# Scale and shift of the context rows, table powers and hold factors read from PSUM; all squares of x summed by TensorE

## The chip, the cores and the metric

One core of one Trainium2 chip runs the whole program. The metric is device time in microseconds (us). The five engines of a core are TensorE (PE: matmuls, and PEld for its weight loads), VectorE (DVE), ScalarE (ACT), GpSimd (POOL) and SyncE (SP, which here only issues DMAs). Each runs its own instructions in program order; semaphores order them against each other. SBUF is the large working memory. PSUM has 8 banks of 512 fp32 columns on 128 partitions; column c of the buffer `PS` lies in bank c // 512.

## What is computed

One layer of a generator over 1024 latent tokens and 256 context tokens of 1024 channels. Its token mixer is a state-space layer (S5) in both directions: 64 groups of 16 channels, 64 complex states each. The part that matters here:

```
mod = silu_c @ ada_w[i] + ada_b[i]                       # shift, scale, gates (6 x 1024)
xn  = rmsnorm(x, norm1_g)   * (1 + sc1)  + sh1           # latent rows
cn  = rmsnorm(ctx, norm1_g) * (1 + csc1) + csh1          # context rows
lam_bar = exp(lam * dt);  B_bar = (lam_bar - 1) / lam * B    # zero-order hold
h_t = lam_bar * h_{t-1} + B_bar u_t                      # scan; the latent scan starts from the context's end
y   = Re(C h);  out = gelu(y + d_skip * u);  GLU with glu_w;  x += g1 * out
x  += g2 * (relu(h @ w1 + b1)^2 @ w2 + b2)               # h from rmsnorm and the second modulation
```

The MLP is 1024 x 4096 twice, and its products take most of the time after the scan.

## The kernel before

Tokens are taken in chunks of 8, so the scan runs over 128 latent and 32 context chunks, 160 columns in all. Channels lie on partitions in 8 blocks j of 8 groups. x stands as `xu(j)`, 128 x 1280 per block (8 groups of 160 columns), context in the first 16 columns of each half. The first 300 us do the following.

1. **Sums of squares.** `squares(j)` (ScalarE, L148) squares a block into one of four buffers that `sqb` names; `sum_squares(j)` (TensorE, L154) adds it up into `ssq`, in PSUM bank 1, by 8 matmuls, each two rows in the trace. Two pairs of squares are first added by GpSimd (L174), so that six blocks go through TensorE. VectorE makes the token scale `R` of the sums (L314 to L322; `R` is in bank 5), and `scale_x(j)` (L326) applies it.
2. **Hold factors and B_bar.** L199 to L207 make two 128 x 64 factors; `b_bar` (L219 to L226) applies them to B in two pieces of 8 instructions (44 groups, then 20). ScalarE copies powers of lam_bar out (`pt` and `pg`, L193 to L210), and L261 on VectorE waits for the last of these.
3. **Tables.** `e_products(j, half)` (L280 to L284, five 128 x 512 instructions) multiplies powers by B_bar; five of the sixteen halves run on VectorE, the rest on GpSimd. `turn_e` transposes each on TensorE (L294), and ScalarE copies it into the table of block j (L296).
4. **Modulation.** Conditioning products (`cond1`, L301) end in `mb` in bank 7 (L424). VectorE makes the vector `md` (L429, L430), TensorE spreads it over partitions (L433), ScalarE copies it to `mu` (L437). `mod_lat` (ScalarE, L445) and `mod_ctx(j)` (VectorE, L450, two 128 x 256 instructions) apply it.
5. **The loop over j.** `states(j, g)` (TensorE, L488 to L490, one call for each of 8 groups; ScalarE copies out at L491 and L492), then `ups(j)` on VectorE: the upper steps of the scan tree (L466 to L469), with `mod_ctx(j + 2)` at its end. The first piece of `ups(j)` needs groups 0 to 3, the second groups 4 to 7. Between groups stand `turn_e` of later tables, `mod_lat(j + 1)`, and `cond2_next` (L401: four matmuls of the other conditioning columns into bank 7 from 512 KB that ScalarE's queue loads), at the places in `C2AT`: after groups 3 and 7 for j < 3, after 7 for j = 3, after 1, 4 and 6 later. In j = 5 to 7 `k_blocks`, `k_mm` and `k_evac` add other tables, and VectorE's `k_finish` (L578 to L581, three 16 x 128 instructions) closes one; SP then stores it.
6. **The scan** follows at L265, on VectorE, then gates, GLU and MLP on TensorE.

The order of each engine's work is the order of the Python text. Where two engines touch one PSUM bank, the program's semaphores order them. The loop of item 5 reads:

```
    for j in range(8):
        for g in range(8):
            states(j, g)
...
            if (j, g) in C2AT:
                cond2_next()
        mc = mod_ctx(j + 2) if j + 2 < 8 else []
        chained(ups(j), mc)
```

Of the kernel before, what the change touches and what calls it, by code (L numbers as in the profile page):

```python
# [10 lines left out]
OP = mybir.AluOpType  # L11
# [32 lines left out]
DVE_E = ((0, 0), (0, 1), (1, 0), (1, 1), (2, 0))  # L44
# [3 lines left out]
def kernel(ctx, tc, cst, bc, x, xl, ada_w, glu_w, w1, w2, out):  # L48
    nc = tc.nc
    V, S, P, PE, SP = nc.vector, nc.scalar, nc.gpsimd, nc.tensor, nc.sync  # L50
# [6 lines left out]
    UT = sp.tile([128, 2560], F32, name="UT")  # L57
# [3 lines left out]
    E2 = [sp.tile([128, 2048], F32, name=f"E2_{j}", tag=f"r2_{j}") for j in range(8)]  # L61
    PS = pp.tile([128, 4096], F32, name="PS")
# [6 lines left out]
    def vw(ap, *dims):  # L69

        if len(dims) == 1:
            return ap
        names = "abcdef"[:len(dims)]
        return ap.rearrange("p (%s) -> p %s" % (" ".join(names), " ".join(names)),
                            **{names[i]: dims[i] for i in range(len(dims))})

    def size(dims):
        n = 1
        for d in dims:
            n *= d  # L80
        return n

    def at(tile_, off, *dims):
        return vw(tile_[:, off:off + size(dims)], *dims)

    def sb(off, *dims):
        assert R3 + off + size(dims) <= R3 + NR3
        return at(T, R3 + off, *dims)

    def bank(i, n=512, o=0):  # L90
        return PS[:, 512 * i + o:512 * i + o + n]
# [6 lines left out]
    def C(name, *dims):  # L98
        o, k = CO[name]
        return at(T, o, *(dims or (k,)))  # L100
# [14 lines left out]
    ETM = 8192  # L115
# [4 lines left out]
    def xu(j, *dims):  # L120
        return at(X1, XU + 1280 * j, *(dims or (8, 2, 80)))
# [20 lines left out]
    exb = C("ex")[:, None, :].to_broadcast([128, 64, NPOW])  # L142
    ssq = bank(1, 160)
    sqt = [at(E2[5], 0, 1280), at(E2[6], 0, 1280), at(E2[7], 0, 1280), at(X0, 2048, 1280)]
    sqb = (0, 1, 2, 3, 1, 3, 0, 2)

    def squares(j):
        S.activation(sqt[sqb[j]], xu(j, 1280), AF.Square)  # L148

    def sum_squares(j):  # L150

        a = vw(sqt[sqb[j]], 8, 160)
        for g in range(8):
            PE.matmul(ssq, C("sel"), a[:, g], start=(j, g) == (0, 0), stop=(j, g) == (7, 7))  # L154
# [13 lines left out]
    V.scalar_tensor_tensor(kk, ang, -1.0, ang, op0=OP.mult, op1=OP.max)  # L168
    S.activation(tb, ang, AF.Sin)
    S.activation(kk, kk, AF.Sin, scale=-1.0, bias=hpi)  # L170
    for j in (0, 2):
        squares(j)
        squares(j + 1)
        P.tensor_tensor(sqt[sqb[j]], sqt[sqb[j]], sqt[sqb[j + 1]], op=OP.add)  # L174
        sum_squares(j)
    V.tensor_scalar(sc, sc, 1.0, None, op0=OP.add)
    V.reciprocal(sc, sc)
# [2 lines left out]
    q = [at(UT, KT + 192 + 64 * i, 64) for i in range(6)]  # L180
# [8 lines left out]
    pt = [sb(PT + 512 * i, 64, 8) for i in range(3)]  # L189
# [5 lines left out]
    for j in range(4, 8):  # L195
        squares(j)
        sum_squares(j)

    V.tensor_scalar(q[0], pwr[:, :, 1], 1.0, None, op0=OP.subtract)  # L199
    V.tensor_tensor(q[3], pwi[:, :, 1], aim, op=OP.mult)  # L200
    V.tensor_tensor(q[2], q[0], are, op=OP.mult)
    V.tensor_tensor(q[4], pwi[:, :, 1], are, op=OP.mult)
    V.tensor_tensor(q[2], q[2], q[3], op=OP.add)
    V.tensor_tensor(q[3], q[0], aim, op=OP.mult)
    V.tensor_tensor(q[2], q[2], q[1], op=OP.mult)
    V.tensor_tensor(q[4], q[4], q[3], op=OP.subtract)
    V.tensor_tensor(q[3], q[4], q[1], op=OP.mult)  # L207
    for i, pw in ((0, pwr), (1, pwi)):
        S.copy(pg[i][fw], pw[fw, :, 0:8])
        S.copy(pg[i][bw], pw[bw, :, 7::-1])  # L210
    br, bi, bd_, bs = (sb(o, 64, 16) for o in (BR, BI, S1, S2))

    def b_bar(a, b):

        gs = slice(a, b)
        n = b - a
        kre, kim = (q[i][:, gs, None].to_broadcast([128, n, 16]) for i in (2, 3))
        t1, t2 = (at(E2[4], 704 * i, n, 16) for i in range(2))
        V.tensor_tensor(t1, br[:, gs], kre, op=OP.mult)  # L219
        V.tensor_tensor(t2, bi[:, gs], kim, op=OP.mult)  # L220
        V.tensor_tensor(bd_[:, gs], bi[:, gs], kre, op=OP.mult)
        V.tensor_tensor(bi[:, gs], br[:, gs], kim, op=OP.mult)
        V.tensor_tensor(br[:, gs], t1, t2, op=OP.subtract)
        V.tensor_tensor(bi[:, gs], bi[:, gs], bd_[:, gs], op=OP.add)
        V.tensor_tensor(bs[:, gs], br[:, gs], bi[:, gs], op=OP.add)
        V.tensor_tensor(bd_[:, gs], bi[:, gs], br[:, gs], op=OP.subtract)  # L226

    b_bar(20, 64)
    V.tensor_tensor(pt[2], pt[0], pt[1], op=OP.add)
    b_bar(0, 20)  # L230


# [3 lines left out]
    TA, TB = 2432, 2960  # L236
# [34 lines left out]

    def e_products(j, hlf):

        eng, tm = (V, at(UT, 0, 5, 512)) if (j, hlf) in DVE_E else (P, sb(ETM, 5, 512))
        er, ei, t = (vw(tm[:, i], 4, 16, 8) for i in (2 * hlf, 2 * hlf + 1, 4))
        gs = slice(8 * j + 4 * hlf, 8 * j + 4 * hlf + 4)
        sh = [128, 4, 16, 8]
        pr, pi, ps_ = (v[:, gs, None].to_broadcast(sh) for v in pt)
        b, d, s = (v[:, gs, :, None].to_broadcast(sh) for v in (br, bd_, bs))
        eng.tensor_tensor(ei, ps_, b, op=OP.mult)  # L280
        eng.tensor_tensor(t, pi, s, op=OP.mult)
        eng.tensor_tensor(er, ei, t, op=OP.subtract)
        eng.tensor_tensor(t, pr, d, op=OP.mult)
        eng.tensor_tensor(ei, ei, t, op=OP.add)  # L284
        return er, ei

    def e_turn(j, hlf, er, ei):
        for pr_ in range(2):
            b = bank(2 + nev[0] % 2)
            nev[0] += 1  # L290
            for gg in range(2):
                g = 2 * pr_ + gg
                for c, e in ((0, er), (1, ei)):
                    PE.transpose(b[:, 128 * (2 * gg + c):128 * (2 * gg + c) + 128],  # L294
                                 e[:, g].rearrange("p h t -> p (h t)"), ident)
            S.copy(at(E2[j], 256 * (4 * hlf + 2 * pr_), 512), b)  # L296
# [9 lines left out]
    def pool_products(j, hlf):  # L306
        pool_e[j, hlf] = e_products(j, hlf)

    R = bank(5, 160, 256)

    v_, r_, t_ = (at(GX, 160 * i, 160) for i in range(3))

# [4 lines left out]
    def token_scale():  # L317
# [3 lines left out]
        V.tensor_tensor(t_, t_, r_, op=OP.mult)  # L321
        V.scalar_tensor_tensor(R, t_, 1.5, r_, op0=OP.add, op1=OP.mult)  # L322

    def scale_x(j):
        xv = xu(j, 8, 160)
        V.tensor_tensor(xv, xv, R[:, None].to_broadcast([128, 8, 160]), op=OP.mult)  # L326

    tp = {}

    def dve_products(j, hlf):  # L330
        tp[j, hlf] = e_products(j, hlf)

    def turn_e(j, hlf):
        e_turn(j, hlf, *(tp if (j, hlf) in DVE_E else pool_e)[j, hlf])
# [47 lines left out]
    def aw2(n):  # L382
        if n in C2X:
            return at(GX, 0, 1024)
        if n >= C2C and n % 3 == C2C % 3:
            return at(X0, 2048, 1024)
        return sb(AW2[n % 2 if n < C2C else (n - C2C) % 3 - 1], 1024)

    def load_aw2(n, eng=SP):
        if n < 32:  # L390
            part, k = 2 + n // 8, n % 8
            eng.dma_start(out=aw2(n), in_=ada_w[128 * k:128 * k + 128, 1024 * part:1024 * part + 1024])
# [41 lines left out]
    mu = at(T, CO["sel"][0], 8, 2, 8, 2)  # L434
    load_aw2(0)
    load_aw2(1)
    S.copy(mu, vw(bank(6, 256), 8, 2, 8, 2))  # L437
    turn_e(5, 0)
    pool_products(6, 0)
    scale_x(3)  # L440
# [5 lines left out]

    def mod_ctx(j):
        xv = xu(j)[:, :, :, 0:16]
        sc_, sh_ = (mu[:, :, i, j, 1:2][:, :, :, None].to_broadcast([128, 8, 2, 16]) for i in (1, 0))
        return [lambda: V.tensor_tensor(xv, xv, sc_, op=OP.mult), lambda: V.tensor_tensor(xv, xv, sh_, op=OP.add)]  # L450

    def save_u(j):
# [97 lines left out]
    def ksr(j, o, *dims):  # L550
        r = 32 + 64 * (j % 2)
        return sb(KS + o, *dims)[r:r + 16]
# [22 lines left out]
    def k_finish(j, eng=V):  # L575

        k0, kf, dj = ksr(j, 0, 8, 15, 16)[:, :, 7], ksr(j, 1920, 8, 16), ksr(j, 2048, 8, 16)
        eng.tensor_tensor(dj, ident[32:48, None, 32:48].to_broadcast([16, 8, 16]),  # L578
                        C("dg")[32:48, 8 * j:8 * j + 8, None].to_broadcast([16, 8, 16]), op=OP.mult)
        eng.tensor_tensor(kf, kf, dj, op=OP.add)  # L580
        eng.tensor_tensor(k0, k0, kf, op=OP.add)  # L581
        kd = KD[j].rearrange("(h t g c) -> t h g c", h=16, t=8, g=8)
        for t in range(8):
            SP.dma_start(out=kd[t], in_=ksr(j, 0, 8, 240)[:, :, 16 * (7 - t):16 * (7 - t) + 128])  # L584


    for g in range(8):
        mod_lat(0, g)
    woven(mod_ctx(0))
    save_u(0)  # L590
    turn_e(2, 0)
# [81 lines left out]
    for q in range(1, 40):  # L673
        if q - 8 in KSTEP[:-1]:
            k_finish(3 + KSTEP.index(q - 8))
        if q in KSTEP:
            j = 3 + KSTEP.index(q)
# [117 lines left out]
    load_u(0)  # L795
    load_m8(2)
    k_finish(7, P)
    load_u(1)
    load_m8(3)
# [286 lines left out]
    t1, t2, t4 = ([(at(W, o + 1024 * k, 512), at(W, o + 1024 * k + 512, 512)) for k in range(4)] for o in (0, 4096, 8192))  # L1086
# [209 lines left out]
    for u in range(1, 5):  # L1296
        for m in range(21):
            t = 14 * (u - 1)
# [112 lines left out]
    for p in range(7, len(L)):  # L1411
        b, i = L[p]
        t = p - len(L)
# [79 lines left out]
    for d in range(8):  # L1493
        o = acc[:, d, toks[1]]
        S.activation(o, o, AF.Identity, scale=C("fg")[:, d:d + 1])
    rb = norm_rows(r_, 2, toks[1])
    for d in range(8):
        o = acc[:, d, toks[1]]
# [64 lines left out]
```

## Time and profile before

| | us |
|---|---|
| median of 3 runs (1109.08 to 1112.32) | 1109.23 |
| the profiled execution | 1112.36 |
| its span (first to last instruction) | 1110.6 |
| busy: TensorE / VectorE / GpSimd / ScalarE | 953.8 / 917.9 / 607.1 / 552.0 |

Mean granted TensorE clock 0.931 of full speed. Times below are microseconds from the start of the span.

### The profile page before, as it was taken

How to read it: one execution, taken by the hardware profiler on the slowest of the kernel's cores; microseconds unless marked ns; L12 is line 12 of the kernel's file. 1: busy time of each engine (PE TensorE's matmuls, PEld its weight loads, DVE VectorE, ACT ScalarE, POOL GpSimd, SP SyncE). 2: the span in 40 equal slices, each digit the busy share in tenths (PEclk: the TensorE clock that was granted, in tenths of full speed). 3: DMA queues.
4: the chain of work that ended last, by engine and by line, in shares of the span. 5: the costliest groups of instructions: out<-in, count | busy, mean ns of one | idle time of the engine just before them, and what ended most of it. 6: DMA issues, size and time to landing. Idle time of an engine off the chain costs nothing.

```text
span 1110.6 us, 15184 instructions
## 1 busy us (share of the span) xinstructions
PE 953.8 (86%) x5244; PEld 782.1 (70%) x5244; DVE 917.9 (83%) x1393; ACT 552.0 (50%) x1012; POOL 607.1 (55%) x413
## 2 busy tenths in 40 slices
PE   3468676656799989789999999997799999999995
PEld 3337565535688867568888888885578788888885
DVE  8999999999984677789666665656979899999997
ACT  7147475334974456745656454544434243434313
POOL 3787899907373553254423232234858677777803
PEclk9778798776899999899999999998999999999998
DMA  9413354486576601156444535358354363625104
GB/s 383 177 39 129 124 168 132 97 227 190 182 237 208 227 19 47 58 189 199 161 153 139 174 133 180 115 189 283 143 173 140 100 213 87 226 75 174 36 1 152
DMA packets 104637, 168.85 MB, mean 152 GB/s; under 512 B 7664, under 2 KB 61936, under 8 KB 103152
## 3 DMA queue, kind: packets, MB, share of 16 engines
q1 hardware_dynamic: 100128, 153.20, 42.1%
q10 hardware_dynamic: 4432, 14.68, 3.9%
q8 instruction: 41, 0.67, 0.2%
q14 instruction: 36, 0.29, 0.1%
HBM read 120.40 MB, written 47.45 MB: 151 GB/s over the span
## 4 chain that ended last, share of the span: by engine, by line
PE 51%; DVE 28%; ACT 6%; DMA 6%; issue 5%; SPq 1%; POOL 1%; ACTq 0%; DVEq 0%; POOLq 0%
PE PS L773 16%; PE PS L774 16%; PE PS L772 16%; DVE X L469 2%; DMA DY<-X 2%; DVE X L468 2%; DVE z L923 2%; DVE PS L467 1%; DVE PS L466 1%; DVE X L450 1%; SPq L584 1%; DMA T<-DY 1%; DVE PS L699 1%; DVE W L923 1%; ACT T L724 1%
## 5 line engine op out<-in xcount | busy, mean ns | idle before, releaser
L773 PE MATMUL PS<-z,W 128*128 128x512 f32 (+1 forms) x422 | 165.5, 392 | 7.2 <-DVE z L923 7.2
L772 PE MATMUL PS<-z,W 128*128 128x512 f32 (+1 forms) x422 | 165.4, 392 | 0.0
L774 PE MATMUL PS<-z,W 128*128 128x512 f32 (+1 forms) x394 | 153.7, 390 | 0.0
L1343 DVE SCALAR_TENSOR_TENSOR T<-PS,T 128x512 f32<-128x512 f32 x160 | 112.3, 739 | 16.2 <-PE PS L774 13.4
L773 PE MATMUL PS<-W 128*128 128x512 f32 (+1 forms) x254 | 100.0, 394 | 9.8 <-DVE W L923 9.8
L772 PE MATMUL PS<-W 128*128 128x512 f32 (+1 forms) x254 | 99.2, 391 | 2.4 <-ACT W L926 2.4
L773 PEld LDWEIGHTS PS<-z,W 128*128 128x128 f32 x422 | 80.8, 192 | 25.5 <-DVE z L923 9.3
L772 PEld LDWEIGHTS PS<-z,W 128*128 128x128 f32 x422 | 80.7, 191 | 16.3
L774 PE MATMUL PS<-W 128*128 128x512 f32 (+1 forms) x226 | 87.9, 389 | 0.0
L774 PEld LDWEIGHTS PS<-z,W 128*128 128x128 f32 x394 | 75.5, 192 | 15.3 <-DVE W L824 0.2
L923 DVE TENSOR_TENSOR z<-z 128x512 fp32r<-128x512 f32 x57 | 79.2, 1422 | 0.0
L774 PE MATMUL PS<-z,A 128*128 128x512 f32 x198 | 77.0, 389 | 0.0
L923 DVE TENSOR_TENSOR W<-W 128x512 fp32r<-128x512 f32 x52 | 69.8, 1376 | 8.0 <-ACT W L926 8.0
L774 PE MATMUL PS<-W,A 128*128 128x512 f32 x194 | 75.5, 389 | 0.0
L488 PE MATMUL PS<-X,E 128*64 128x160 f32 x256 | 50.8, 341 | 26.6 <-DVE X L450 18.7
L1173 DVE TENSOR_TENSOR T<-T,PS 128x512 f32<-128x512 f32 x64 | 42.9, 685 | 34.7 <-PE PS L774 34.0
L773 PE MATMUL PS<-z,A 128*128 128x512 f32 x170 | 66.2, 390 | 2.1 <-DVE z L923 2.1
L1201 POOL TENSOR_TENSOR T<-T 128x512 f32<-128x512 f32 x25 | 36.1, 1444 | 56.2 <-ACT T L1144 48.1
L772 PE MATMUL PS<-z,A 128*128 128x512 f32 x170 | 66.3, 390 | 0.0
L926 ACT CAST W<-T 128x512 fp32r<-128x512 f32 (+1 forms) x46 | 32.9, 718 | 65.3 <-POOL T L1268 38.9
L773 PEld LDWEIGHTS PS<-W 128*128 128x128 f32 x254 | 48.7, 192 | 23.4 <-DVE W L923 14.1
L923 POOL TENSOR_TENSOR W<-T,W 128x768 fp32r<-128x768 f32 (+1 forms) x24 | 43.6, 1819 | 38.5 <-ACT W L926 38.5
(329 smaller groups left out, 2778.2 us busy)
## 6 DMA issues: line engine op xcount, KB each, us to landing
YD<-T SPq DMA_DIRECT2D x87, 256.0 KB, 2.3
z<-YD SPq DMA_DIRECT2D x57, 256.0 KB, 3.4
W<-YD SPq DMA_DIRECT2D x52, 256.0 KB, 4.8
T<-in_w_dram SPq DMA_DIRECT2D x9, 1024.0 KB, 5.8
T<-in_ada_w_dram ACTq DMA_DIRECT2D x17, 512.0 KB, 4.0
UT<-in_w_dram SPq DMA_DIRECT2D x8, 1024.0 KB, 5.8
T<-in_w_dram SPq DMA_DIRECT2D x20, 384.0 KB, 6.4
UT<-in_w_dram SPq DMA_DIRECT2D x15, 384.0 KB, 4.2
```

The source lines that it names most:

```text
L450: return [lambda: V.tensor_tensor(xv, xv, sc_, op=OP.mult), lambda: V.tensor_tensor(xv, xv, sh_, op=OP.add)]
L468: lambda: eng.tensor_tensor(out_, out_, ta, op=OP.add),
L469: lambda: eng.tensor_tensor(out_, out_, tb_, op=OP.add)]
L488: PE.matmul(b[0:64, c], e[:, g, c, 0:64], uj[:, g], start=True, stop=True)
L772: PE.matmul(o, wt[0], xt[0], start=start, stop=False)
L773: PE.matmul(o, wt[0], xt[1], start=False, stop=False)
L774: PE.matmul(o, wt[1], xt[0], start=False, stop=stop)
L923: eng.tensor_tensor(lo, src, hi.bitcast(F32), op=OP.subtract)
L926: S.copy(vw(to[0][:, 0:size(dims)], *dims) if dims else to[0], src)
L1173: V.tensor_tensor(to, x_, o, op=OP.add)
L1201: P.tensor_tensor(o, x_, z_, op=op)
L1343: V.scalar_tensor_tensor(o, src, g2[:, d:d + 1], o, op0=OP.mult, op1=OP.add)
```

## The change

These values move from SBUF to PSUM: the first two powers tables (`ptv`, two ScalarE copies into bank 1), the products' temporary `t` on VectorE's share, the hold factors (`hold`, bank 7) and two temporaries of `b_bar`, context's scale and shift (`muc`, one more ScalarE copy, bank 7) and `k_finish`'s temporaries (bank 6). `R` moves from bank 5 to bank 7. GpSimd's two adds of squares go; TensorE sums all eight blocks.

```diff
-    sqb = (0, 1, 2, 3, 1, 3, 0, 2)
+    sqb = (0, 1, 2, 3, 0, 1, 2, 3)
...
-    for j in (0, 2):
+    for j in range(4):
         squares(j)
-        squares(j + 1)
-        P.tensor_tensor(sqt[sqb[j]], sqt[sqb[j]], sqt[sqb[j + 1]], op=OP.add)
         sum_squares(j)
...
+    ptv = [vw(bank(1, 160, 160 + 160 * i), 20, 8) for i in range(2)]
+    for i in range(2):
+        S.copy(ptv[i], pt[i][:, 0:20])
+
+    hold = [PS[:, 3616 + 64 * i:3680 + 64 * i] for i in range(2)]
...
-    V.tensor_tensor(q[2], q[2], q[1], op=OP.mult)
+    V.tensor_tensor(hold[0], q[2], q[1], op=OP.mult)
...
-    V.tensor_tensor(q[3], q[4], q[1], op=OP.mult)
+    V.tensor_tensor(hold[1], q[4], q[1], op=OP.mult)
...
-        kre, kim = (q[i][:, gs, None].to_broadcast([128, n, 16]) for i in (2, 3))
-        t1, t2 = (at(E2[4], 704 * i, n, 16) for i in range(2))
+        kre, kim = (h[:, gs, None].to_broadcast([128, n, 16]) for h in hold)
+        t1, t2, t3 = at(E2[4], 0, n, 16), *(vw(PS[:, o:o + 16 * n], n, 16) for o in (1024, 2048))
...
+        t = vw(PS[:, TA:TA + 512] if on_v else tm[:, 4], 4, 16, 8)
...
+        pr, pi, ps_ = (v[:, gs, None].to_broadcast(sh) for v in (*(ptv if on_v else pt[:2]), pt[2]))
...
-    R = bank(5, 160, 256)
+    R = bank(7, 160, 32)
...
+    muc = vw(bank(7, 128, 384), 8, 2, 8)
     S.copy(mu, vw(bank(6, 256), 8, 2, 8, 2))
+    S.copy(muc, vw(bank(6, 256), 8, 2, 8, 2)[:, :, :, :, 1])
...
-        sc_, sh_ = (mu[:, :, i, j, 1:2][:, :, :, None].to_broadcast([128, 8, 2, 16]) for i in (1, 0))
+        sc_, sh_ = (muc[:, :, i, j:j + 1][:, :, :, None].to_broadcast([128, 8, 2, 16]) for i in (1, 0))
...
+        if eng is V:
+            r = 32 + 64 * (j % 2)
+            dj, ks = (vw(PS[r:r + 16, o:o + 128], 8, 16) for o in (3200, 3328))
```

No instruction of the loop changes its place on its engine; what changes there is what it waits for. On TensorE, before, the conditioning matmuls (L401) wait for their load alone, and the first state product of block 3 (its table is `E_3`) is what waits for VectorE, which is to say for `mod_ctx(3)`:

```order
L488 MATMUL PS<-X_69,E_2_72 64x160
L489 MATMUL PS<-X_69,E_2_72 64x2x64
L490 MATMUL PS<-X_69,E_2_72 64x2x16
L401 MATMUL PS<-T 1x256 [waits DMAHW3_49]
L401 MATMUL PS<-T 1x256 x3
L488 MATMUL PS<-X_69,E_3_73 64x160 [waits DVE_49,Activation_49]
```

Now (L401 has become L406, L488 to L490 are L495 to L497) the conditioning matmuls that stand after group 3 of block 2 wait for VectorE as well, and by its count for the second instruction of `mod_ctx(3)`, which reads `muc` in bank 7 and stands at the end of `ups(1)`:

```order
L495 MATMUL PS<-X_69,E_2_72 64x160
L496 MATMUL PS<-X_69,E_2_72 64x2x64
L497 MATMUL PS<-X_69,E_2_72 64x2x16
L406 MATMUL PS<-GX,T 1x256 [waits DMAHW1_49,DVE_49]
L406 MATMUL PS<-GX,T 1x256 x3
L495 MATMUL PS<-X_69,E_2_72 64x160 [waits Activation_49]
```

So the wait for `mod_ctx(3)` has moved forward by half a block: groups 4 to 7 of block 2 now stand behind it. The same holds at six more places, by the semaphore counts: (0, 3) waits for `mod_ctx(1)`, (1, 3) for `mod_ctx(2)`, (3, 7) for `mod_ctx(4)`, (4, 1) for `mod_ctx(5)`, (5, 1) for `mod_ctx(6)` and (6, 1) for `mod_ctx(7)`.

The second place is ScalarE's start, from the second half of the squares (L148) to the copies of powers whose end L261 (now L264) on VectorE waits for. Before:

```order
L148 ACTIVATE E_6_76<-X_69 128x1280 [waits DMAHW6_49,Pool_49]
L148 ACTIVATE X_68<-X_69 128x1280 [waits DMAHW7_49,Pool_49]
L148 ACTIVATE E_5_75<-X_69 128x1280 [waits DMAHW0_49,PE_49]
L148 ACTIVATE E_7_77<-X_69 128x1280 [waits DMAHW1_49,PE_49]
L209 COPY T<-E_2_72 64x512
L210 COPY T<-E_2_72 64x512
L209 COPY T<-UT 64x512
L210 COPY T<-UT 64x512
```

And of the change:

```order
L148 ACTIVATE E_7_77<-X_69 128x1280 [waits DMAHW0_49,PE_49,Activation_49]
L148 ACTIVATE X_68<-X_69 128x1280 [waits DMAHW1_49,PE_49,Activation_49]
L199 COPY PS<-T 128x160 [waits PE_49,Activation_49]
L199 COPY PS<-T 128x160 [waits Activation_49]
L212 COPY T<-E_2_72 64x512
L213 COPY T<-E_2_72 64x512
L212 COPY T<-UT 64x512
L213 COPY T<-UT 64x512
```

The copy to `ptv` (L199), in bank 1 beside `ssq`, waits for TensorE's last sum of squares, and the four copies of powers now stand behind it.

## Rows read from the trace of the kernel before

**Rows 1.** Busy us by stage: PE, PEld, DVE, ACT, POOL; PEclk; DMA share; GB/s.

```profile
85.00:212.00 127.00, 89.31 (x1110) 74.93 (x1112) 117.76 (x192) 74.81 (x250) 112.50 (x96) 0.86 0.43 134
```

**Rows 2.** VectorE's timeline to 64 us: start, duration, line, operation.

```profile
15.07 2.93 DVE L200 TENSOR_TENSOR UT<-UT,T 128x64 f32<-128x64 f32 x1
...
29.85 1.36 DVE L220 TENSOR_TENSOR E<-T,UT 128x320 f32<-128x320 f32 x1
...
41.35 0.71 DVE L261 TENSOR_TENSOR T<-T 128x512 f32<-128x512 f32 x1
...
43.66 1.55 DVE L281 TENSOR_TENSOR UT<-T 128x512 f32<-128x512 f32 x1
```

**Rows 3.** GpSimd's timeline at its first add.

```profile
14.97 2.94 POOL L174 TENSOR_TENSOR E<-E,E 128x1280 f32<-128x1280 f32 x1 [10.40 <-ACT E L148]
```

**Rows 4.** ScalarE's timeline, three places.

```profile
12.48 3.57 ACT L148 ACTIVATE E<-X 128x1280 f32<-128x1280 f32 x3
...
27.37 0.66 ACT L210 COPY T<-UT 64x512 f32<-64x512 f32 x1
...
163.51 0.38 ACT L491 COPY X<-PS 128x264 f32<-128x264 f32 x1
```

**Rows 5.** TensorE's timeline, the last sums of squares.

```profile
28.38 4.51 PE L154 MATMUL PS<-E,T 128*128 128x160 f32 x32
```

**Rows 6.** VectorE's timeline, 75 to 124 us.

```profile
75.26 1.47 DVE L326 TENSOR_TENSOR X<-X,PS 128x1280 f32<-128x1280 f32 x1
...
96.86 0.71 DVE L466 TENSOR_TENSOR PS<-X,PS 128x528 f32<-128x528 f32 x1 [1.04 <-ACT X L491]
...
108.00 0.70 DVE L466 TENSOR_TENSOR PS<-X,PS 128x528 f32<-128x528 f32 x1
...
123.08 0.70 DVE L466 TENSOR_TENSOR PS<-X,PS 128x528 f32<-128x528 f32 x1
```

**Rows 7.** VectorE's timeline, 150 to 212 us.

```profile
150.31 0.70 DVE L466 TENSOR_TENSOR PS<-X,PS 128x528 f32<-128x528 f32 x1
...
163.63 0.70 DVE L466 TENSOR_TENSOR PS<-X,PS 128x528 f32<-128x528 f32 x1
...
177.19 1.25 DVE L578 TENSOR_TENSOR T<-T 16x128 f32<-16x128 f32 x1
...
211.01 0.28 DVE L265 COPY PS<-PS 128x128 f32<-128x128 f32 x1
```

**Rows 8.** VectorE's groups by line and shape, 80 to 212 us: busy, mean ns, idle before.

```profile
L450 DVE TENSOR_TENSOR X<-X,T 128x256 f32<-128x256 f32 x16 | 18.5, 1157 | 0.1
...
L581 DVE TENSOR_TENSOR T<-T 16x128 f32<-16x128 f32 x3 | 3.6, 1199 | 0.2
...
L466 DVE TENSOR_TENSOR PS<-X,PS 128x224 f32<-128x224 f32 x8 | 3.2, 396 | 1.2 <-DVE X L468 0.5
```

**Rows 9.** Waits over 62 to 213 us: total us, times, longest.

```profile
PE PS L401 <- DVE PS L267: 7.5, 1, 7.5
```

**Rows 10.** TensorE's timeline in the loop.

```profile
100.88 0.61 PE L401 MATMUL PS<-GX,T 128*1 128x256 f32 x8
...
104.42 1.09 PE L294 MATMUL PS<-T 128*128 128x128 f32 x8
...
108.23 0.32 PE L488 MATMUL PS<-X,E 128*64 128x160 f32 x1 [2.18 <-DVE X L450]
...
123.31 0.50 PE L488 MATMUL PS<-X,E 128*64 128x160 f32 x1 [6.98 <-DVE X L450]
...
127.90 1.09 PE L294 MATMUL PS<-T 128*128 128x128 f32 x8
...
139.15 1.03 PE L401 MATMUL PS<-T 128*1 128x256 f32 x8
...
152.84 1.03 PE L401 MATMUL PS<-T 128*1 128x256 f32 x8
```

**Rows 11.** TensorE's granted clock: stretch, busy, PEclk, DMA share, GB/s.

```profile
120.00:122.00 2.00, 0.00 (x0) 0.57 0.00 0
```

More of the change, by code (lines that the diff above doesn't have):

```diff
@@ L216, in b_bar @@
         n = b - a
-        kre, kim = (q[i][:, gs, None].to_broadcast([128, n, 16]) for i in (2, 3))
-        t1, t2 = (at(E2[4], 704 * i, n, 16) for i in range(2))
+        kre, kim = (h[:, gs, None].to_broadcast([128, n, 16]) for h in hold)
+        t1, t2, t3 = at(E2[4], 0, n, 16), *(vw(PS[:, o:o + 16 * n], n, 16) for o in (1024, 2048))
         V.tensor_tensor(t1, br[:, gs], kre, op=OP.mult)
         V.tensor_tensor(t2, bi[:, gs], kim, op=OP.mult)
-        V.tensor_tensor(bd_[:, gs], bi[:, gs], kre, op=OP.mult)
+        V.tensor_tensor(t3, bi[:, gs], kre, op=OP.mult)
         V.tensor_tensor(bi[:, gs], br[:, gs], kim, op=OP.mult)
         V.tensor_tensor(br[:, gs], t1, t2, op=OP.subtract)
-        V.tensor_tensor(bi[:, gs], bi[:, gs], bd_[:, gs], op=OP.add)
+        V.tensor_tensor(bi[:, gs], bi[:, gs], t3, op=OP.add)
         V.tensor_tensor(bs[:, gs], br[:, gs], bi[:, gs], op=OP.add)
@@ L272, in e_products @@
     def e_products(j, hlf):
-        eng, tm = (V, at(UT, 0, 5, 512)) if (j, hlf) in DVE_E else (P, sb(ETM, 5, 512))
-        er, ei, t = (vw(tm[:, i], 4, 16, 8) for i in (2 * hlf, 2 * hlf + 1, 4))
+        on_v = (j, hlf) in DVE_E
+        eng, tm = (V, at(UT, 0, 4, 512)) if on_v else (P, sb(ETM, 5, 512))
+        er, ei = (vw(tm[:, i], 4, 16, 8) for i in (2 * hlf, 2 * hlf + 1))
+        t = vw(PS[:, TA:TA + 512] if on_v else tm[:, 4], 4, 16, 8)
         gs = slice(8 * j + 4 * hlf, 8 * j + 4 * hlf + 4)
         sh = [128, 4, 16, 8]
-        pr, pi, ps_ = (v[:, gs, None].to_broadcast(sh) for v in pt)
+        pr, pi, ps_ = (v[:, gs, None].to_broadcast(sh) for v in (*(ptv if on_v else pt[:2]), pt[2]))
         b, d, s = (v[:, gs, :, None].to_broadcast(sh) for v in (br, bd_, bs))
@@ L577, in k_finish @@
         k0, kf, dj = ksr(j, 0, 8, 15, 16)[:, :, 7], ksr(j, 1920, 8, 16), ksr(j, 2048, 8, 16)
+        ks = kf
+        if eng is V:
+            r = 32 + 64 * (j % 2)
+            dj, ks = (vw(PS[r:r + 16, o:o + 128], 8, 16) for o in (3200, 3328))
         eng.tensor_tensor(dj, ident[32:48, None, 32:48].to_broadcast([16, 8, 16]),
                         C("dg")[32:48, 8 * j:8 * j + 8, None].to_broadcast([16, 8, 16]), op=OP.mult)
-        eng.tensor_tensor(kf, kf, dj, op=OP.add)
-        eng.tensor_tensor(k0, k0, kf, op=OP.add)
+        eng.tensor_tensor(ks, kf, dj, op=OP.add)
+        eng.tensor_tensor(k0, k0, ks, op=OP.add)
         kd = KD[j].rearrange("(h t g c) -> t h g c", h=16, t=8, g=8)
```

## The prediction, made before the change was run

> **What bounds the kernel now.** I read busy time by stage first, then VectorE's timeline up to the scan, then what TensorE waits for in the loop over j. From 85 to 212 us VectorE is busy 117.8 of 127 us, TensorE 89.3, GpSimd 112.5 [rows 1]: VectorE sets the pace up to the scan, and GpSimd works beside it nearly all the time. The scan starts at 211.01 [rows 7]; everything behind it is ordered after it, so I take each us that its start moves as one us of the total. All but a few short instructions of the change lie before that point.
>
> Two kinds of VectorE instruction are slow here. With both operands in SBUF they stretch beside GpSimd: L200, 64 columns, takes 2.93 [rows 2] while GpSimd's add takes 2.94 over the same time [rows 3]; a product of 512 columns takes 1.55, L220 of 320 columns 1.36 [rows 2], and the sixteen instructions of `mod_ctx` (L450, 256 columns) 1.157 in the mean [rows 8]. With one operand in PSUM they do not: L466 takes 0.70 or 0.71 for 528 columns [rows 6] and 0.396 for 224 [rows 8], with GpSimd just as busy. So a contended instruction that gets a PSUM operand falls to about 0.72 (512 columns), 0.5 (320), 0.43 (256), estimates from these two widths.
>
> **The change up to the loop.** GpSimd's adds go, so L200 and its twin fall from 2.93 to under 0.3 (as 128 columns take 0.28 [rows 7]): 5.3 us. Five of the contended instructions of `b_bar`'s second piece fall from about 1.36 to 0.5: 4.3. VectorE would be ready for L261 at 41.35 - 9.6 = 31.8 [rows 2].
>
> It cannot go on then. Three squares take ScalarE 3.57 from 12.48, so the first ends at 13.7 [rows 4], and TensorE need no longer wait for the add, which ends at 17.9 [rows 3]. But it has 128 rows to do in place of 96, and 32 rows take 4.51 [rows 5]. Before, 17.9 to 32.9 were 15.0 for 96 rows; now 19.5, ending at 33.2. The two copies to `ptv` wait for that end, since they write the bank of the sums, and ScalarE's four copies of powers stand behind them (0.66 each, before done at 28.0 [rows 4]). With 0.3 for each `ptv` copy (bounds: nothing, or the 0.66 of the wider copy) they end at 36.6. VectorE, 9.6 us ahead, loses 4.9 of it: 4.8 remain.
>
> Five table halves run on VectorE. Beside GpSimd five instructions of about 1.5 become one of 1.5 and four of 0.73: 3.1 less. That holds for the first, third and fifth; the second and fourth ran while GpSimd was idle and gain nothing, and I count 1 us lost on the fourth. Ahead by 4.8 + 3.1 + 3.1 - 1.0 = 10.0. Now two new waits: `scale_x(2)` writes from `R` in bank 7 and waits for the conditioning products there, about 1.6; `scale_x(3)`, which ran at 75.26 [rows 6] with no wait, waits for the copy to `muc`, which comes after `md`, TensorE's spreading matmuls and two copies: 2.9 (both estimates; bounds 2 and 7 together). Left: 5.5. Fifth half: 8.6. `mod_ctx(0)` saves 2 x 0.73 (1.157 less 0.43): 10.1, of which TensorE's last transposes, which had ended before it, take 0.8. The first states come 9.3 earlier, and with them the second piece of `ups(0)`, at 96.86 before [rows 6]: 87.5. This sum has an uncertainty of about 3 us.
>
> **The loop, where it is given back.** From that second piece to the next block's first is 108.00 - 96.86 = 11.1 [rows 6], with two `mod_ctx` instructions in it; now 9.7, so `ups(1)` starts at 97.2. A block in which VectorE waits for nothing took 163.63 - 150.31 = 13.3 [rows 7]; now 11.9.
>
> But the conditioning matmuls in bank 7 now wait for `mod_ctx(j + 2)` of the block before, which is the last thing that VectorE does ahead of `ups(j)`. Behind them on TensorE, in order, stand the remaining groups of block j, whose copies the second piece of `ups(j)` needs. So in j = 1, 2, 4, 5, 6 TensorE no longer works ahead: VectorE ends block j - 1, then TensorE does the rest of block j's groups, then VectorE goes on. The block takes D(j) + 9.7, where D is the time from the matmuls' start to ScalarE's copy of the last group.
>
> That such a wait goes by bank and not by columns is in the trace of before: the same matmuls once waited 7.5 us for L267 on VectorE [rows 9], which reads other columns of bank 7. The Trainium skill ("PSUM — Partial Sum Buffer", section on bank collisions) states the rule that speaks against this change: PSUM is to be guarded by bank and quadrant, since another address of the same bank still collides. By addresses the loop would lose nothing and the total be about 1080; by banks the sum is what follows.
>
> D from rows. With TensorE fast, conditioning takes 0.54 and four groups 3.0 (100.88 to 104.42), 0.75 a group; after an idle stretch conditioning takes 0.96 (1.03 in its row, less overlap) and four groups 4.6 (123.31 to 127.90), 1.15 a group [rows 10]. The clock behind it: granted 0.57 in the mean over 120 to 122, with TensorE idle [rows 11], that is on its way from 2.4 to 1.2 GHz; it was idle 6.98 ahead of 123.31 [rows 10]. In the change TensorE idles 5 to 10 us ahead of each of the five waits, so I take each D with a slow start and a fast end. ScalarE's copies add 0.7.
> - D(1) = 0.96 + 4.0 + 0.7 = 5.7. D(2) has a transposed table more (1.09 in rows 10): 6.7.
> - D(4) has six groups, two slow, and two more conditioning parts: 0.96 + 2 x 1.15 + 4 x 0.75 + 1.2 + 0.7 = 8.2.
> - D(5) stands in the trace, slow start included: 152.84 [rows 10] to ScalarE's copy at 163.51 + 0.38 [rows 4] is 11.05; with the semaphore 11.3. D(6) has the same work.
>
> Starts of `ups(j)`: j = 2 at 97.2 + 5.7 + 9.7 = 112.6 (before 123.08 [rows 6]); 3 at 129.0; 4, without a stall, at 140.9 (150.31); 5 at 158.8 (163.63); 6 at 158.8 + 11.3 + 9.7 = 179.8, where before VectorE was at 177.19 [rows 7]. From there to the scan: 11.3, in which `k_finish(0)` is hidden, 8.9 (9.7 without `mod_ctx`), a `k_finish` of 0.9 (its instructions took 1.199 beside GpSimd [rows 8], alone 0.3), 11.1 and 0.9 again, 33.1: the scan starts at 212.9 against 211.01.
>
> That is 1.9 us later: 1114.3 for the profiled execution, which took 1112.36 and lies 3.1 above the median; against the median of 1109.23 it is **1111**.
>
> **Rivals.**
> 1. *The waits bind, but TensorE stays fast*, or its idle stretches end sooner. D falls by 1.5, 1.5, 1.2, 0.8 and 0.8: 5.8 us, total 1105. For it: after 2.18 us of idle, at 108.23, a state product took 0.32. Against it: after 6.98 it took 0.50 [rows 10].
> 2. *The change does what it says and the waits cost nothing.* Five blocks at 11.9 from 97.2, then 25: scan at 181.7, total 1080. For it: VectorE is busy nearly throughout, so all that is saved there counts. Against it: the order of TensorE's queue and [rows 9].
> 3. *Slower*: TensorE stays slow through all of D, since it now works in short bursts. Every group at 1.15, every conditioning part at 0.96, the tables in j = 5 and 6 likewise: D grows by 0.6, 1.1, 2.3, 2.6 and 2.6, total 1111 + 9 = 1120. It decides from the point where the clock comes back only after the last group. For it: in the stretch after 123.31 four whole groups take 4.6. Against it: the next rows there, 1.09 for the transposes at 127.90, are as fast as at 104.42 [rows 10].
>
> **How the numbers follow.** A run of this kernel tells about 0.3% (3.3 us) from no change: below 1105.9 is faster, above 1112.6 slower. Forecast 0.42, by itself 1107 to 1115; rival 1 0.22, rival 2 0.08, rival 3 0.28. Faster: rival 2, over half of rival 1 and a tail of the forecast, 0.24. Slower: nearly all of rival 3 and a quarter of the forecast, 0.35. Same: 0.41. The range runs from 1098 (rival 1 with 3 us more saved up to the loop and some of rival 2) to 1120; outside it is most of rival 2 and a tail of rival 3.
>
> **What would show it.** L200 at 0.3 and L450's successor at 0.43 show the contention gone; VectorE idle before L264 until ScalarE's copies, near 36.6, shows the first stall; `ups(1)` starts near 97. In the loop VectorE must idle ahead of the second piece in j = 1, 2, 4, 5, 6 for D less the first piece's 2.3, about 30 us in all, released by ScalarE's L498, and TensorE's conditioning matmuls by L457. If VectorE has no such idle time, or the matmuls wait for loads alone, the forecast is wrong; if the idle time is there and the clock in D is full, rival 1; if it is half throughout, rival 3.

## The result: slower by 0.9%, and the profile after

| | before | after |
|---|---|---|
| median, us | 1109.23 | 1120.94 (1115.91 to 1121.58, 5 runs) |
| ratio to before, 95% interval | | 1.0088 (1.0063 to 1.0114) |
| profiled execution / its span, us | 1112.36 / 1110.6 | 1120.36 / 1118.6 |
| start of the scan in the profile, us | 211.01 | 220.92 |

The forecast was 1111, no change or a little slower, with a range from 1098 to 1120. The change costs 11.7 us by the medians and 9.8 by the ratio (0.0088 of 1110). Lines of the changed kernel stand 3 to 11 higher: L261 is L264, L401 is L406, L450 is L457, L466 is L473, L491 is L498, L566 is L573.

The window that answers to [rows 1] (busy us of PE, PEld, DVE, ACT, POOL, then PEclk, DMA share, GB/s):

```profile
85.00:212.00 127.00, 79.20 (x972) 65.65 (x972) 84.00 (x161) 64.11 (x216) 102.73 (x90) 0.80 0.40 124
```

VectorE was busy 117.8 of these 127 us and is now busy 84.0: what it saved stands there as idle time. Its timeline after, with the idle time before an instruction and who ended it in brackets, answers to [rows 2, 6, 7]:

```profile
15.31 0.21 DVE L204 TENSOR_TENSOR UT<-UT,T 128x64 f32<-128x64 f32 x1
...
36.85 1.24 DVE L264 TENSOR_TENSOR T<-T 128x512 f32<-128x512 f32 x1 [5.28 <-ACT T L213]
...
67.95 1.49 DVE L331 TENSOR_TENSOR X<-X,PS 128x1280 f32<-128x1280 f32 x1 [3.30 <-ACT PS L444]
...
102.02 0.71 DVE L473 TENSOR_TENSOR PS<-X,PS 128x528 f32<-128x528 f32 x1 [3.67 <-ACT X L498]
...
119.41 0.71 DVE L473 TENSOR_TENSOR PS<-X,PS 128x528 f32<-128x528 f32 x1 [5.34 <-ACT X L498]
...
149.94 0.71 DVE L473 TENSOR_TENSOR PS<-X,PS 128x528 f32<-128x528 f32 x1 [2.34 <-ACT X L498]
...
172.63 0.71 DVE L473 TENSOR_TENSOR PS<-X,PS 128x528 f32<-128x528 f32 x1 [4.06 <-ACT X L498]
...
182.60 0.35 DVE L589 TENSOR_TENSOR PS<-T 16x128 f32<-16x128 f32 x1
...
196.99 0.71 DVE L473 TENSOR_TENSOR PS<-X,PS 128x528 f32<-128x528 f32 x1 [5.19 <-ACT X L498]
...
220.92 0.30 DVE L268 COPY PS<-PS 128x128 f32<-128x128 f32 x1
```

Read from the top: L204 was L201 before, the twin of the contended L200, and takes 0.21 in place of 2.93. L264 stands still 5.28 us until ScalarE's copies of powers. `scale_x(3)` waits 3.30 for the copy to `muc`. Then the second piece of `ups(j)` waits in j = 1, 2, 4, 5 and 6 (L473, released by ScalarE's copy of a state group), 2.34 to 5.34 us each; in j = 4, 5, 6 the first piece waits too, 3.89, 6.49 and 5.88. `k_finish(0)` starts at 182.60, the scan at 220.92. The waits summed over 28 to 220 us (total, times, longest):

```profile
PE PS L406 <- DVE X L457: 41.6, 6, 10.0
...
DVE PS L473 <- ACT X L498: 40.1, 10, 6.5
...
DVE T L264 <- ACT T L213: 5.3, 1, 5.3
```

TensorE's conditioning matmuls wait 41.6 us for `mod_ctx`, six times, and VectorE then waits 40.1 us for state groups. Of these, 3.3 us fall in j = 0, where the conditioning matmuls did not have to wait, and 36.9 behind the waits in j = 1, 2, 4, 5 and 6; the sixth wait, 1.66 us after (3, 7), holds VectorE up nowhere. Before, L401 waited for VectorE once, 7.5 us [rows 9], and VectorE waited for ScalarE 1.04 us in `ups(0)` [rows 6] and 1.30 us in `ups(7)`.

### The profile page after: what moved, and what is told of

Same layout as the page of the kernel before. It is cut to its first block, busy times and chain, and to the rows that moved or that the text cites. A ratio compares the mean times of both kernels' runs of the same rounds, so it can differ in the third digit from the quotient of the medians.

```text
span 1118.6 us, 15256 instructions
## 1 busy us (share of the span) xinstructions
PE 962.0 (86%) x5276; PEld 789.3 (71%) x5276; DVE 878.4 (79%) x1393; ACT 553.6 (49%) x1015; POOL 590.3 (53%) x411
## 4 chain that ended last, share of the span: by engine, by line
PE 57%; DVE 22%; ACT 8%; DMA 5%; issue 4%; POOL 3%; SPq 1%; DVEq 0%; POOLq 0%; ACTq 0%
PE PS L784 16%; PE PS L785 16%; PE PS L783 16%; DVE X L476 2%; DMA DY<-X 2%; DVE X L475 2%; PE PS L154 2%; PE PS L573 2%; DVE PS L474 2%; DVE PS L473 2%; DVE z L934 1%; PE PS L495 1%; DMA T<-in_ada_w_dram 1%; ACT T L735 1%; PE PS L406 1%
## 5 line engine op out<-in xcount | busy, mean ns | idle before, releaser
L934 DVE TENSOR_TENSOR z<-z 128x512 fp32r<-128x512 f32 x57 | 75.7, 1361 | 0.0
L785 PE MATMUL PS<-W,A 128*128 128x512 f32 x194 | 75.5, 389 | 0.0
L784 PE MATMUL PS<-W,A 128*128 128x512 f32 x166 | 64.6, 389 | 0.0
L783 PE MATMUL PS<-W,A 128*128 128x512 f32 x166 | 64.6, 389 | 0.0
```

What stands on the lines that cost most here:

```text
L783: PE.matmul(o, wt[0], xt[0], start=start, stop=False)
L784: PE.matmul(o, wt[0], xt[1], start=False, stop=False)
L785: PE.matmul(o, wt[1], xt[0], start=False, stop=stop)
L934: eng.tensor_tensor(lo, src, hi.bitcast(F32), op=OP.subtract)
```

## The experiments

Two theories. Theory A: the loss is the wait of the conditioning matmuls for `mod_ctx`, which exists since `muc` lies in their bank; the rest of the change gains. Theory B: the copy in PSUM gains, and the loss comes from the other parts (longer sums on TensorE, copies in ScalarE's queue, the clock).

**The copy in another bank.** Only 96 columns of bank 6 are free through the loop, so six blocks read it and two read SBUF as before the change.

```diff
-    muc = vw(bank(7, 128, 384), 8, 2, 8)
+    muc = vw(bank(6, 96, 416), 8, 2, 6)
-    S.copy(muc, vw(bank(6, 256), 8, 2, 8, 2)[:, :, :, :, 1])
+    S.copy(muc, vw(bank(6, 256), 8, 2, 8, 2)[:, :, :, 0:6, 1])
-        sc_, sh_ = (muc[:, :, i, j:j + 1][:, :, :, None] ...
+        sc_, sh_ = ((muc[:, :, i, j:j + 1] if j < 6 else mu[:, :, i, j, 1:2])[:, :, :, None] ...
```

> The change with the context's scale and shift in bank 6 in place of bank 7, for six of the eight blocks (96 columns are free there; blocks 6 and 7 read SBUF as before the change). Theory (the wait of the conditioning matmuls for mod_ctx, by bank 7, is what was lost): the five stalls of the loop go, VectorE starts ups(1) near 93, since scale_x(3) no longer waits 3.3 us for the copy either, and the scan near 181; total 1083 us (1076 to 1095). Rival (the loss comes from TensorE's clock and the longer sums of squares, whatever bank is read): 1115 to 1122.

Measured 1087.64 us, ratio 0.9795 (0.9781 to 0.9810). TensorE's groups by line, 80 to 188 us (busy, mean ns, idle before):

```profile
L406 PE MATMUL PS<-T 128*1 128x256 f32 x128 | 10.2, 392 | 1.6 <-DMA T<-in_ada_w_dram 1.6
...
L406 PE MATMUL PS<-GX,T 128*1 128x256 f32 x16 | 1.2, 377 | 0.0
```

None of L406's idle time is put down to VectorE any more; it is 1.6 us, for a load. VectorE's timeline:

```profile
63.82 1.49 DVE L331 TENSOR_TENSOR X<-X,PS 128x1280 f32<-128x1280 f32 x1 [1.25 <-PE PS L429]
...
188.18 0.30 DVE L268 COPY PS<-PS 128x128 f32<-128x128 f32 x1
```

`scale_x(3)`'s wait is gone too; `scale_x(2)`'s (63.82) is left. The scan starts at 188.18, 32.7 us sooner than with the copy in bank 7, although two of the eight blocks read SBUF again. The choice of that bank decides the sign of the whole change. Against the estimate of 181 the scan is 7 us late, and the total is 5 us above the 1083 expected, inside the range. The trace shows where most of the 7 us lie, if the prediction's sizes are taken for this part: the second piece of `ups(7)` waits 2.12 us for ScalarE; `k_finish`, whose first instruction stays slow, takes 1.8, 1.5 and 1.6 us where the prediction had 0.9; and `ups(6)` and `ups(7)`, without that wait, take about 11.8 us each where it had 11.1.

```profile
157.53 1.05 DVE L589 TENSOR_TENSOR PS<-T 16x128 f32<-16x128 f32 x1
...
177.05 0.71 DVE L473 TENSOR_TENSOR PS<-X,PS 128x528 f32<-128x528 f32 x1 [2.12 <-ACT X L498]
```

**No copy.** `mod_ctx` reads SBUF as before, the rest of the change stays.

```diff
-    muc = vw(bank(7, 128, 384), 8, 2, 8)
-    S.copy(muc, vw(bank(6, 256), 8, 2, 8, 2)[:, :, :, :, 1])
...
-        sc_, sh_ = (muc[:, :, i, j:j + 1][:, :, :, None] ...
+        sc_, sh_ = (mu[:, :, i, j, 1:2][:, :, :, None] ...
```

> The change without the PSUM copy of the context's scale and shift: mod_ctx reads SBUF as before, all other parts stay. Theory: no stalls in the loop, but mod_ctx takes about 1.16 us an instruction again beside GpSimd; ups(1) near 96, scan near 189, total 1089 us (1083 to 1097). Rival (the other parts lose by themselves): above 1109.

Measured 1095.04 us, ratio 0.9867 (0.9852 to 0.9881): the other parts gain, and theory B's second half falls. The total is 6 us above the one expected, inside its range. `mod_ctx` in that run (its line is L455 there):

```profile
L455 DVE TENSOR_TENSOR X<-X,T 128x256 f32<-128x256 f32 x15 | 17.3, 1154 | 0.1
```

At 1.154 us an instruction it is as slow as before the change [rows 8]; that costs 8 us against the copy in bank 6 (0.9867 - 0.9795 of 1110).

**The copy alone, in bank 7, on the kernel before.**

```diff
+    muc = vw(bank(7, 128, 384), 8, 2, 8)
     S.copy(mu, vw(bank(6, 256), 8, 2, 8, 2))
+    S.copy(muc, vw(bank(6, 256), 8, 2, 8, 2)[:, :, :, :, 1])
-        sc_, sh_ = (mu[:, :, i, j, 1:2][:, :, :, None] ...
+        sc_, sh_ = (muc[:, :, i, j:j + 1][:, :, :, None] ...
```

> The kernel before with that copy in bank 7 alone. Theory: mod_ctx falls to 0.41 us an instruction, the conditioning matmuls wait for it, and without the gains of the other parts the loop's loss stands alone: scan near 232, total 1128 us (1122 to 1134). Rival (the copy gains and other parts lose): 1092 to 1098, since 16 instructions get 0.73 us shorter.

Measured 1132.47 us, ratio 1.0212 (1.0190 to 1.0233). Every `mod_ctx` instruction is 0.74 us shorter, and the kernel is 22 us slower; the scan starts at 232.21, where 232 was expected. TensorE's groups, 84 to 232 us:

```profile
L401 PE MATMUL PS<-T 128*1 128x256 f32 x128 | 11.6, 438 | 28.4 <-DVE X L452 26.9 <-DMA T<-in_ada_w_dram 1.5
...
L401 PE MATMUL PS<-GX,T 128*1 128x256 f32 x24 | 2.7, 531 | 11.9 <-DVE X L452 11.9
```

L401 waits 26.9 + 11.9 us for VectorE's L452, the `mod_ctx` of that kernel. Theory A holds from both sides.

**Sums of squares away from the copies of the powers.** On top of the copy in bank 6:

```diff
-    ssq = bank(1, 160)
+    ssq = bank(6, 160)
```

> As the run with the scale and shift in bank 6, and the sums of squares in bank 6 too, away from the copies of the powers in bank 1. Theory: the copies no longer wait for the last sum, VectorE's stall of 5.3 us ahead of L264 goes, total 4 to 5 us under that run, near 1079 us. Rival (TensorE's sums end at 33 anyway and hold the later work): equal to that run within 1 us.

Measured 1082.87 us, ratio 0.9753 (0.9739 to 0.9768), 4.7 us under the first run by the ratios, as expected. VectorE no longer waits ahead of L264; one wait is left before the loop, 2.06 us ahead of `scale_x(2)`:

```profile
57.49 1.49 DVE L331 TENSOR_TENSOR X<-X,PS 128x1280 f32<-128x1280 f32 x1 [2.06 <-PE PS L429]
...
182.28 0.30 DVE L268 COPY PS<-PS 128x128 f32<-128x128 f32 x1
```

**TensorE kept busy while it waits.** The change as it is, with matmuls whose results nobody reads ahead of five of the waits:

```diff
+            for _ in range({(1, 3): 5, (2, 3): 5, (4, 1): 9, (5, 1): 8, (6, 1): 8}.get((j, g), 0)):
+                PE.matmul(bank(2), ident, at(E2[j], 0, 512), start=True, stop=True)
             if (j, g) in C2AT:
                 cond2_next()
```

> The change, with 5, 5, 9, 8 and 8 extra matmuls of 512 columns (estimate 0.93 us each at full speed, their results not used) ahead of the conditioning matmuls after (1,3), (2,3), (4,1), (5,1) and (6,1), so that TensorE works through most of the time in which it waits for mod_ctx and is granted the full clock behind it. Theory: the waits stay, D(1), D(2), D(4), D(5), D(6) fall from 5.8, 7.4, 8.4, 12.7 and 14.4 by 1.5, 1.5, 1.4, 2.6 and 2.4 us: total 1111 us (1108 to 1115); what is left above the run with the copy in bank 6 is the order of the two engines alone. Rival (the clock costs nothing, only the order does): 1120 or above.

Measured 1111.26 us, ratio 0.9998 (0.9982 to 1.0014). TensorE's timeline:

```profile
90.57 4.56 PE L636 MATMUL PS<-E,T 128*128 128x512 f32 x10 [0.52 <-ACT E L301]
...
95.94 0.61 PE L406 MATMUL PS<-GX,T 128*1 128x256 f32 x8 [0.81 <-DVE X L457]
...
110.10 0.61 PE L406 MATMUL PS<-GX,T 128*1 128x256 f32 x8 [1.50 <-DVE X L457]
```

The conditioning matmuls take 0.61 behind each of the five waits, where they took 1.03. D(1), D(2), D(4), D(5) and D(6) fall by 1.6, 2.3, 0.2, 2.3 and 2.9 us, 9.2 in all, and the scan starts at 211.69, 9.2 us sooner than in the change. So about 10 us (1.0088 - 0.9998 of 1110) of what the wait costs is the half clock behind it, and doing useless work gains them back.

The sum came out as expected, but not each term: D(4) was to fall by 1.4 us and fell by 0.2. There TensorE idled only 2.11 us behind the extra matmuls and the conditioning matmuls were fast, yet right behind them it was granted the half clock (0.53 over 137.95 to 141.6), and the state products took 0.47 to 0.53, as behind the waits of the change:

```profile
137.39 0.61 PE L406 MATMUL PS<-T 128*1 128x256 f32 x8 [2.11 <-DVE X L457]
...
137.94 0.51 PE L495 MATMUL PS<-X,E 128*64 128x160 f32 x1
```

Behind the other four waits the granted clock was 1.00. The other 22 or 23 us, down to the first run's 0.9795, are by difference the order of the two engines, with `scale_x(3)`'s 3.1 us and what is left of the half clock in block 4 among them.

**What the other parts are worth**, each taken back from the version of the fourth run. GpSimd's adds as before the change (its loop and `sqb`):

> The version with scale and shift and the sums of squares in bank 6, with GpSimd's two adds of squares as before the change. Theory: L203 and its twin wait 2.9 us each for the adds again, 5.3 us, of which VectorE's 2.1 us wait for the conditioning products takes up to 2: total 1086 to 1088 us against 1082.9. Rival (eight blocks on TensorE cost as much as they save): equal within 1 us.

Measured 1085.46 us, 0.9759 (0.9742 to 0.9776): not told apart from 0.9753. Since the scan started 4.1 us later in its profile, base and variant were run once more on one chip.

> The version with scale and shift and the sums of squares in bank 6, once more, as the base for the two runs beside it on the same chip: ratio to before 0.975.

> That version with GpSimd's two adds of squares, once more, beside its base on the same chip. The scan started 4.1 us later than in the base's profile, so by theory 3 to 4 us above the base; by the rival (what TensorE's longer sums cost equals what the adds cost) within 1 us of it.

Measured 1082.56 us, 0.9753 (0.9739 to 0.9768), and 1085.76 us, 0.9783 (0.9766 to 0.9800). The adds cost about 3 us by the medians of this pair, as theory had it, and the scan starts 2.8 us later; but the intervals overlap and the first pair showed 0.7 us by the ratios, so the cost is not clear of noise.

`k_finish` with its temporaries in SBUF as before the change:

```diff
-        if eng is V:
-            r = 32 + 64 * (j % 2)
-            dj, ks = (vw(PS[r:r + 16, o:o + 128], 8, 16) for o in (3200, 3328))
```

> The same version with k_finish's temporaries in SBUF as before the change. Theory: three times three 16x128 instructions at about 1.1 us beside GpSimd in place of 0.3, all on VectorE's path to the scan now that nothing waits in the loop: 6 to 7 us more, 1089 to 1090 us. Rival (hidden behind TensorE or ScalarE): equal within 1 us.

Measured 1086.24 us, 0.9772 (0.9751 to 0.9793): 2 us more by the ratios and 3 by the medians, with overlapping intervals, and the scan starts at 185.45, 3.2 us later: at most half of what was expected. Its second and third instruction, two of three calls in the window (busy, mean ns):

```profile
L588 DVE TENSOR_TENSOR T<-T 16x128 f32<-16x128 f32 x2 | 2.3, 1174 | 0.1
...
L589 DVE TENSOR_TENSOR T<-T 16x128 f32<-16x128 f32 x2 | 2.4, 1180 | 0.1
```

They are slow again (L588, L589), but the first one was often slow in both (0.28 to 1.04 here, 0.76 to 1.10 in the fourth run): it multiplies two SBUF operands in the changed kernel as well (L589 there, below), so less was saved than I had counted. And 1.2 us of the loss hide in VectorE's wait ahead of the second piece of `ups(7)`, 1.99 in the fourth run and 0.75 here, so the rival holds in part:

```profile
171.02 0.71 DVE L473 TENSOR_TENSOR PS<-X,PS 128x528 f32<-128x528 f32 x1 [1.99 <-ACT X L498]
...
172.91 0.71 DVE L473 TENSOR_TENSOR PS<-X,PS 128x528 f32<-128x528 f32 x1 [0.75 <-ACT X L498]
```

Powers, products' temporary, hold factors and `b_bar`'s temporaries in SBUF as before the change:

> The same version with the powers, the products' temporary, the hold factors and B_bar's temporaries in SBUF as before the change. Theory: 4.3 us in B_bar and 3.1 in each of the table halves that run beside GpSimd come back, 9 to 12 us: 1092 to 1095 us. Rival (TensorE's turns hold the tables): 1083 to 1087.

Measured 1092.71 us, 0.9833 (0.9815 to 0.9850): 9 us more, at the lower end of what was expected.

**The first products' bank.** On top of the fourth run:

```diff
-    mb = vw(bank(7, 32), 16, 2)
+    mb = vw(bank(6, 32, 256), 16, 2)
```

> The version with scale and shift and the sums of squares in bank 6, and the conditioning products of the first part (mb) moved from bank 7 to bank 6 too, so that scale_x(2), which reads the token scale in bank 7, waits for no matmul. Theory: VectorE's wait of 2.1 us ahead of scale_x(2) goes, but md needs the same matmuls one instruction later, so 0 to 2 us less than that version. Rival (the wait only moves on to md): equal within 0.5 us.

Measured 1080.33 us, 0.9741 (0.9721 to 0.9760), 2 us under its base by the medians, with overlapping intervals. VectorE waits neither for `scale_x(2)` nor for `md` any more, but the scan starts at 181.66 against 182.28 and 182.50 in the two runs of the base, so a gain is not shown clear of noise. By its median it is the fastest version here, by the ratios 39 us under the change and 29 under the kernel before.

## Why the prediction was right or wrong

**Up to the loop: right.** ScalarE's copies were forecast at 36.6 and L264 started at 36.85. `ups(1)` was forecast at 97.2 and started at 96.15, as the second `mod_ctx` instruction ended. The two waits for bank 7, 1.23 and 3.30 us, are the 1.6 and 2.9 of the estimate.

**`mod_ctx`: right.** 0.415 us an instruction against the estimate of 0.43; the groups 80 to 221 us:

```profile
L457 DVE TENSOR_TENSOR X<-X,PS 128x256 f32<-128x256 f32 x14 | 5.8, 415 | 0.0
...
L589 DVE TENSOR_TENSOR PS<-T 16x128 f32<-16x128 f32 x3 | 1.6, 524 | 0.1
```

**The wait by bank: right**, in kind and place, and shown by the first and third runs. Rival 2, 1080 if the waits cost nothing, did not come; with the copy moved the total was 1087.6.

**The clock: right in kind.** TensorE idled 5.9, 6.0, 10.0, 9.0 and 9.0 us ahead of the five waits, and each time the conditioning matmuls behind took 1.03; behind the sixth wait, 1.66 us, they took 0.61. The granted clock behind the wait ahead of `ups(5)` was at the lower of its two levels, 1.2 GHz (0.50), and then at 2.4 GHz (1.00), so it was not half throughout (stretch, its length, TensorE's busy time, granted clock, DMA share, GB/s):

```profile
160.00:162.00 2.00, 2.00 (x18) 0.50 0.00 0
...
166.00:168.00 2.00, 2.00 (x35) 1.00 0.00 0
```

Rival 1, a fast TensorE at 1105, did not come; kept busy on purpose it gave 1111.

**Starts in the loop** (forecast, measured at the end of the `mod_ctx` ahead, as the first piece itself can wait): `ups(2)` 112.6, 112.0; `ups(3)` 129.0, 129.4; `ups(4)` 140.9, 141.5; `ups(5)` 158.8, 159.9; then the wait ahead of `ups(6)` 179.8, 182.6; the scan 212.9, 220.9. Up to `ups(5)` the sum is right to 1.1 us. Of the 8 us at the scan, 7 are lost behind it.

**The step that failed is the size of D(5) and D(6)**, "11.05; with the semaphore 11.3. D(6) has the same work". Measured are 172.63 - 159.93 = 12.7 and 196.99 - 182.62 = 14.4. D(1) and D(4) came out at 5.7 and 8.4, close to the forecast of 5.7 and 8.2, and D(2) at 7.4 in place of 6.7, since its transposed table was slow too (1.72 in place of 1.09). D(5) was read from a block of before whose slow start was shorter: there the other tables' matmuls were fast again. TensorE's timeline before:

```profile
154.79 1.69 PE L566 MATMUL PS<-E,T 128*48 128x128 f32 x14
```

And after:

```profile
96.29 1.03 PE L406 MATMUL PS<-GX,T 128*1 128x256 f32 x8 [5.90 <-DVE X L457]
...
159.93 1.03 PE L406 MATMUL PS<-T 128*1 128x256 f32 x8 [9.01 <-DVE X L457]
...
162.23 2.95 PE L573 MATMUL PS<-E,T 128*48 128x128 f32 x14
...
167.62 1.69 PE L573 MATMUL PS<-E,T 128*48 128x128 f32 x14
...
182.62 1.03 PE L406 MATMUL PS<-T 128*1 128x256 f32 x8 [9.01 <-DVE X L457]
...
184.92 3.19 PE L573 MATMUL PS<-E,T 128*48 128x128 f32 x14
```

Here the slow stretch reaches into the other tables' matmuls: 14 rows of L573 take 2.95 and 3.19 in place of 1.69. That is a part of rival 3. Its total of 1120 is what came out, but in part by luck: the five D came out 5.4 us over the forecast where rival 3 had 9.2, and a part of the 5.4 is ScalarE's. That part lies in j = 6; ScalarE's timeline after:

```profile
193.83 0.57 ACT L578 COPY T<-PS 16x512 f32<-16x512 f32 x1
...
194.42 0.52 ACT L579 COPY T<-PS 16x448 f32<-16x448 f32 x1
...
195.06 0.74 ACT L412 COPY T<-PS 1x256 f32<-1x256 f32 x2
...
196.57 0.38 ACT L498 COPY X<-PS 128x264 f32<-128x264 f32 x1
```

TensorE had done the last group of j = 6 at about 194.5, but ScalarE's copy of it (196.57) stood behind three copies of the tables and four of a finished part of the conditioning (L412), 2.7 us from 193.83 on, so it came 2.0 us after the group. Such a part ends in j = 6 and none in j = 5, so D(6) does not have the work of D(5). The trace of before showed these copies already, L407, ahead of the copy of the same group at 177.37:

```profile
175.85 0.74 ACT L407 COPY T<-PS 1x256 f32<-1x256 f32 x2
...
177.37 0.38 ACT L491 COPY X<-PS 128x264 f32<-128x264 f32 x1
```

I had looked for what stands behind the wait on TensorE and not at what stands ahead of the copy on ScalarE.

The rest of the 8 us lies in `k_finish` and `ups(7)`: 206.48 to 207.77 is 1.29 for a `k_finish` where I had 0.9, twice, since L589 still has two SBUF operands (0.524 in the mean, 0.62 at worst), `ups(7)` took 11.85 in place of 11.1, and block 6 behind its stall took 9.5 in place of 8.9. The 11.1 was too short by the trace of before as well, where `ups(6)`, the first block without `mod_ctx`, took 11.8 (180.96 to 192.79).

**One us of the scan's start is one us of the end: right within about 2 us by the ratios.** The scan started 9.9 us later and the ratio says 9.8; in the third run 21.2 and 23.5 later, in the fourth 28.7 and 27.4 earlier, in the run with the extra matmuls 0.7 later and 0.2 earlier. A single profiled execution can differ by more: the last of these has a span 5.3 us shorter than before.

**The forecast as a whole** had the mechanism, its place and the stalls, and a sum of +1.9 where +9.9 came at the scan. Because it is the difference of a gain of some 23 us (the first run) and a loss of some 33, a miss of 8 us, over half of it in two blocks, moved the answer from "no change" to slower, at the upper end of the range.

## What to carry to other kernels

Where a program's semaphores order the accesses to PSUM by bank, as here, a value moved into PSUM brings all accesses of its bank into one order across engines, so the bank is to be chosen by who else uses it, and when. Before moving an operand, list the other users of the bank, look up which of them stands early in an in-order queue, and count what is queued behind it: here 16 instructions got 0.74 us shorter, and the waits that their bank brought cost about 33 us. Where such a wait is sized from rows, take the clock that TensorE will have behind it, and add what stands ahead on the engine that copies the results out.

## What the runs showed of the hardware that was not expected

- Useless matmuls paid: with TensorE idle 5.9 to 10 us ahead of each of five waits the ratio was 1.0088, with most of each wait filled by matmuls 0.9998. The granted clock ahead of and behind the wait at 159.93 was 0.50 in the first case (158 to 164 us), and 1.00 behind the same wait in the second (155.6 to 160.6). In one block of five the filling did not hold the clock: after 8 us of extra matmuls and 2.11 us of idle time it was granted 0.53 over 137.95 to 141.6.
- An instruction with a PSUM output and two SBUF inputs can stay slow beside GpSimd: L589 took 0.35 to 0.62 in the change, 0.76 to 1.10 in the fourth run and 0.29 to 1.05 when that version ran once more, while L591 and L592, with one operand in PSUM, took 0.28 to 0.31. GpSimd worked beside all of these. With `k_finish` back in SBUF the first of its three instructions took 0.28 to 1.04, so the output's place shows no gain.
